# Up projection's moving activations in rows of 272 columns, with single buffers for two of the convolution's tiles

## The chip, the cores and the metric

The kernel runs on one core of one Trainium2 chip. The metric is the device time of one execution in microseconds, as the median of several runs. Before the change it is 1212.79 us (three runs, 1211.92 to 1213.15).

## What is computed

One decoder layer over 272 positions (16 meta tokens and 256 of the sequence), model width 2048, everything in float32. Cut to what matters here:

```
u = rmsnorm(h, norm_mix)
proj = u @ w_in                                  # retention and mLSTM heads
mix = concat([ret, hm]) @ w_out
h = h + mix
u = rmsnorm(h, norm_ffn)
up = causal_dwconv(u @ w_up, ffn_conv_w, ffn_conv_b)   # 3 taps, 2 x 5632 channels
gate, val = split(up)
h = h + (silu(gate) * val) @ w_down
return rmsnorm(h)[:, 16:]
```

The meta tokens are dropped at the end, so the up projection is needed for the last 256 positions and for the two before them that the convolution's three taps reach back to: 258 columns (`NQ = 258`, `T = 272`, `T0 = 14`, `SEQ = 256`).

## The kernel before

**Precision.** A float32 product is made of three passes of TensorE in the type float32r: weights and activations are each parted into a high and a low part, and high by high, high by low and low by high are added up in PSUM. `load_w` (L115) loads a half-tile of weights `wraw` (128 partitions x 8 blocks of 128 columns) by a DMA of SyncE's queue, ScalarE copies it to the high part `whi` (L121) and VectorE subtracts to get the low part `wlo` (L123). There are 4 buffers of `wraw` and 5 each of `whi` and `wlo`.

**A half-tile.** `half_tile` (L135) calls `mmk` (L126): for each of 8 blocks k of the contraction a matmul of `whi` with the high activations (L130) and one with the low ones (L131), and after these sixteen the eight of `wlo` with the high activations (L133). That is 24 matmuls; in each, the weights are the stationary operand (128 x 128) and a row of activations, one row per k, is the moving one. `project` (L140) makes an output tile of 128 channels from two such half-tiles, k = 0 to 7 and k = 8 to 15, in one PSUM bank `mmps` of four.

**Three layouts of moving rows.** The heads read `xh` and `xl`, tiles of shape (128, 16, 272): a row of one k has 272 columns, 1088 bytes. Keys and values use all 272; queries and gates of the retention heads, and the mLSTM gates, use the last 258 (`xh[:, k, 14:272]`). The output projection reads `mixh` and `mixl`, of shape (128, 16, 258), in rows of 1032 bytes. The up projection reads `uh` and `ul` (L567, L568), of the same shape (128, 16, 258).

**Stages.** In the order of time: heads (to about 371 us), output projection (16 tiles, to 465), first half of the up projection (44 tiles, each gate tile followed by its value tile), first half of the down projection, second half of the up projection (44 tiles), second half of the down projection, and the last norm. `out_tile` (L577) writes `uh` (ScalarE, L580) and `ul` (VectorE, L581) row by row while the output projection runs, sixteen times each. The 88 tiles of the up projection are 176 half-tiles.

**Behind each tile of the up projection** runs `conv3` (L630): VectorE takes the tile out of PSUM into `cu` with the norm's factor (L633), ScalarE makes the third tap and the bias from it into `gt` or `vt` (L635), and VectorE adds the two other taps, reading `cu` twice more (L637, two instructions). When gate and value are there, ScalarE applies silu to `gt` (L767), VectorE multiplies by `vt` (L768), and the product is parted for the down projection (L744, L746). `cu`, `gt` and `vt` are tiles of the pool `wk2` with two buffers each. They are named at L631 and L634.

**Order.** Each engine takes its instructions in the order of a schedule that is made when the program is built; waits between engines are semaphores. A tile's buffer may be written again when the last reader of its former content is done. Beside the tiles, GpSimd's queue starts early loads for the down projection (L713 to L722), and VectorE transposes `hT` (L628).

**Where the tiles lie.** The pools `hnp`, `up` and `wk2` are stacked on the right side of the on-chip memory, each below the one before. In every partition `hn` begins at byte 212,960, `ul` at 196,448, `uh` at 179,936; `xh` of the heads lay at 165,760 and `xl` at 183,168, `mixh` at 94,656. Buffers of weights lie 4096 bytes apart.

Of the kernel before, what the change touches and what calls it, by code (L numbers as in the profile page):

```python
# [10 lines left out]
F32 = mybir.dt.float32  # L11
F32R = mybir.dt.float32r
# [4 lines left out]
P = 128  # L17
DM = 2048
KT = DM // P
SEQ = 256  # L20
NMETA = 16
T = SEQ + NMETA
T0 = NMETA - 2
NQ = T - T0
# [59 lines left out]
def trunk(ctx: ExitStack, tc: tile.TileContext, io, out: bass.AP):  # L84
    nc = tc.nc

    def pool(name, bufs, **kw):
        return tc.tile_pool(name=name, bufs=bufs, **kw)
# [13 lines left out]
    def pcol(name, i, n=1):  # L102
        a = _COLS[name][0]
        return par[:, a + i : a + i + n]
# [101 lines left out]
    with pool("sq", 1, side="right") as sqp:  # L206
        for k0, k1 in [(0, 1), (1, 2)] + [(k, k + 2) for k in range(2, KT, 2)]:
            n = k1 - k0
# [355 lines left out]
    hn = hnp.tile([P, 2, DM], F32, name="hn")  # L564
    up_cm = pool("up", 1, side="right")
    up = up_cm.__enter__()
    uh = up.tile([P, KT, NQ], F32R, name="uh")  # L567
    ul = up.tile([P, KT, NQ], F32R, name="ul")  # L568
    wk2_cm = pool("wk2", 2, side="right")
    wk2 = wk2_cm.__enter__()  # L570

# [56 lines left out]
            nc.vector.transpose(dst[:, :, t, 32 * i : 32 * (i + 1)], src[:, :, t, a, :])  # L628

    def conv3(ps, f, name):  # L630
        u = wk2.tile([P, NQ], F32, name="cu")  # L631
        nonlocal evacuated
        evacuated = nc.vector.tensor_tensor(out=u, in0=ps[:, :NQ], in1=rstd2, op=ALU.mult)  # L633
        o = wk2.tile([P, SEQ], F32, name=name)  # L634
        nc.scalar.activation(o, u[:, 2:], AF.Identity, scale=pcol("fw", 3 * f + 2), bias=pcol("fb", f))  # L635
        for j in range(2):
            nc.vector.scalar_tensor_tensor(out=o, in0=u[:, j : j + SEQ], scalar=pcol("fw", 3 * f + j), in1=o, op0=ALU.mult, op1=ALU.add)  # L637
        return o
# [85 lines left out]
    for half in range(2):  # L724
# [23 lines left out]
        gt = None  # L748
        for jj in range(NHF):
            j = half * NHF + jj  # L750
            pair = []
            for s in range(2):
# [7 lines left out]
                if 2 * jj + s in begins:  # L760
                    n = begins.index(2 * jj + s)
                    b, q = units[n]
                    running.append(Early(b, half * NQD + q, homes[n], gt))
                    early[b, q] = running[-1].kept
            gt = conv3(pair[0], j, "gt")
            vt = conv3(pair[1], NF + j, "vt")
            nc.scalar.activation(gt, gt, AF.Silu)  # L767
            nc.vector.tensor_tensor(out=gt, in0=gt, in1=vt, op=ALU.mult)  # L768
# [280 lines left out]
```

## Time and profile before

| | |
|---|---|
| median of three runs | 1212.79 us |
| span of the profiled execution, first to last instruction | 1210.4 us |
| TensorE busy | 1198.6 us, 99% |
| VectorE busy | 970.1 us, 80% |
| ScalarE busy | 708.5 us, 59% |
| GpSimd busy | 165.1 us, 14% |
| output projection, a stretch of 94.00 us | TensorE 94.00, VectorE 61.84, ScalarE 55.76 |
| first half of up, a stretch of 242.90 us | TensorE 242.90, VectorE 209.32, ScalarE 130.73 |
| second half of up, a stretch of 246.30 us | TensorE 246.30, VectorE 194.94, ScalarE 134.66 |

The profile shows one execution; its own time on the device isn't listed beside its span, so the 2.39 us between the median and the span stand for what lies around the span. Durations of single matmuls overlap, because matmuls are pipelined: the time that a matmul takes from the others is the distance from its start to the next start, not its own length. In the views of stretches, the number in brackets behind an engine's busy time counts its instructions.

### The profile page before, as it was taken

What the parts mean: (1) busy time and instruction counts of PE and PEld (TensorE: products, weight loads), DVE (VectorE), ACT (ScalarE), POOL (GpSimd) and SP (SyncE); (2) the same over time, 40 slices, a digit from 0 to 9 for tenths busy, and PEclk for the clock granted to TensorE, in tenths of its full rate; (3) what the DMA queues carried; (4) which work ended last, traced back from release to release, by engine and by line L of the source; (5) the groups of instructions that cost most, each with busy time, mean ns of one, the idle gap of its engine ahead of it and who ended that gap; (6) DMA issues with size and microseconds to landing.
All of it is one profiled execution on the core that took longest, in us unless ns stands there. A gap on an engine that the chain in (4) does not pass through costs nothing.

```text
span 1210.4 us, 22758 instructions
## 1 busy us (share of the span) xinstructions
PE 1198.6 (99%) x8956; PEld 1155.6 (95%) x8956; DVE 970.1 (80%) x1444; ACT 708.5 (59%) x963; POOL 165.1 (14%) x228
## 2 busy tenths in 40 slices
PE   9999999999999999999999999999999999999997
PEld 9999999999999999999999997788999999998886
DVE  8877778766775767789888879996798778789897
ACT  8657646656556656555555546665555555556674
POOL 0100001111110211021122210202022112100232
PEclk9999999999999999999999999999999999999999
DMA  8765555656564655766766775959777677755956
GB/s 277 265 220 160 166 189 171 199 175 189 181 193 141 208 178 176 248 220 208 246 225 209 270 268 202 261 200 272 275 252 261 216 245 239 259 177 208 286 179 185
DMA packets 83004, 263.27 MB, mean 218 GB/s; under 512 B 14672, under 2 KB 18896, under 8 KB 82768
## 3 DMA queue, kind: packets, MB, share of 16 engines
q1 hardware_dynamic: 71952, 223.85, 56.4%
q0 software_dynamic: 10368, 37.11, 10.0%
q8 instruction: 70, 1.15, 0.4%
q10 hardware_dynamic: 576, 0.85, 0.2%
q14 instruction: 38, 0.31, 0.1%
HBM read 243.42 MB, written 11.27 MB: 210 GB/s over the span
## 4 chain that ended last, share of the span: by engine, by line
PE 92%; DMA 4%; DVE 2%; issue 1%; ACT 0%; SPq 0%; DVEq 0%; POOL 0%; ACTq 0%; POOLq 0%
PE mmps L130 25%; PE mmps L131 25%; PE mmps L133 24%; PE atps L807 3%; PE atps L808 3%; PE atps L810 2%; PE mmps L842 2%; PE mmps L839 1%; PE mmps L840 1%; PE atps L842 1%; PE atps L840 1%; PE atps L839 1%; DMA wraw<-in_wd 1%; DMA hT<-in_wd 1%; DVE wlo L746 1%
## 5 line engine op out<-in xcount | busy, mean ns | idle before, releaser
L121 ACT CAST whi<-wraw 128x1024 fp32r<-128x1024 f32 x352 | 368.7, 1049 | 316.6 <-PE mmps L131 216.9
L123 DVE TENSOR_TENSOR wlo<-wraw,whi 128x1024 fp32r<-128x1024 f32 x352 | 433.1, 1232 | 71.9 <-ACT whi L121 69.6
L130 PE MATMUL mmps<-uh,whi 128*128 128x258 f32 x1408 | 346.7, 283 | 0.0
L131 PE MATMUL mmps<-ul,whi 128*128 128x258 f32 x1408 | 346.6, 283 | 0.0
L131 PEld LDWEIGHTS mmps<-ul,whi 128*128 128x128 f32 x1408 | 266.6, 189 | 0.1
L130 PEld LDWEIGHTS mmps<-uh,whi 128*128 128x128 f32 x1408 | 266.4, 189 | 0.1
L130 PE MATMUL mmps<-xh,whi 128*128 128x272 f32 (+2 forms) x864 | 219.9, 288 | 0.0
L131 PE MATMUL mmps<-xl,whi 128*128 128x272 f32 (+2 forms) x864 | 218.4, 286 | 0.0
L133 PE MATMUL mmps<-uh,wlo 128*128 128x258 f32 x1408 | 199.0, 283 | 0.0
L133 PEld LDWEIGHTS mmps<-uh,wlo 128*128 128x128 f32 x1408 | 181.3, 189 | 0.0
L131 PEld LDWEIGHTS mmps<-xl,whi 128*128 128x128 f32 x864 | 163.0, 189 | 0.0
L130 PEld LDWEIGHTS mmps<-xh,whi 128*128 128x128 f32 x864 | 162.7, 188 | 0.1
L133 PE MATMUL mmps<-xh,wlo 128*128 128x272 f32 (+2 forms) x864 | 126.8, 286 | 0.0
L133 PEld LDWEIGHTS mmps<-xh,wlo 128*128 128x128 f32 x864 | 114.4, 188 | 0.0
L633 DVE TENSOR_TENSOR cu<-mmps,rstd 128x258 f32<-128x258 f32 x88 | 37.3, 424 | 47.6 <-PE mmps L133 47.1
L746 DVE TENSOR_TENSOR wlo<-hT,whi 128x1024 fp32r<-128x1024 f32 x52 | 62.8, 1236 | 5.6 <-ACT whi L744 5.0
L744 ACT CAST whi<-hT 128x1024 fp32r<-128x1024 f32 x52 | 53.3, 1051 | 23.4 <-DMA hT<-in_wd 5.6
L131 PE MATMUL mmps<-mixl,whi 128*128 128x258 f32 x256 | 63.0, 283 | 0.0
L130 PE MATMUL mmps<-mixh,whi 128*128 128x258 f32 x256 | 62.4, 283 | 0.0
L744 ACT CAST whi<-wraw 128x1024 fp32r<-128x1024 f32 (+1 forms) x52 | 42.1, 835 | 18.5 <-DVE wraw L824 4.8
L807 PE MATMUL atps<-whi,mh 128*128 128x512 f32 (+1 forms) x132 | 50.9, 387 | 2.0 <-ACT whi L121 2.0
L746 DVE TENSOR_TENSOR wlo<-wraw,whi 128x1024 fp32r<-128x1024 f32 (+1 forms) x52 | 51.4, 1014 | 0.8 <-PE mmps L842 0.2
(276 smaller groups left out, 1704.4 us busy)
## 6 DMA issues: line engine op xcount, KB each, us to landing
wraw<-in_wu SPq DMA_DIRECT2D x176, 512.0 KB, 4.4
wraw<-in_wi SPq DMA_DIRECT2D x108, 512.0 KB, 4.2
hT<-in_wd SPq DMA_DIRECT2D x26, 768.0 KB, 4.5
wraw<-in_wd SPq DMA_DIRECT2D x36, 512.0 KB, 5.1
wraw<-in_wo SPq DMA_DIRECT2D x32, 512.0 KB, 3.8
x<-in_wd POOLq DMA_DIRECT2D x14, 768.0 KB, 7.6
hT<-in_wd POOLq DMA_DIRECT2D x12, 768.0 KB, 6.4
hn<-x POOLq DMA_DIRECT2D x27, 256.0 KB, 7.8
```

The source lines that it names most:

```text
L121: nc.scalar.copy(hi, raw)
L123: nc.vector.tensor_tensor(out=lo, in0=raw, in1=hi.bitcast(F32), op=ALU.subtract)
L130: nc.tensor.matmul(ps, hi[:, k, :], xh(kk), start=kk == first, stop=False)
L131: nc.tensor.matmul(ps, hi[:, k, :], xl(kk), start=False, stop=False)
L133: nc.tensor.matmul(ps, lo[:, k, :], xh(kk), start=False, stop=kk == last)
L633: evacuated = nc.vector.tensor_tensor(out=u, in0=ps[:, :NQ], in1=rstd2, op=ALU.mult)
L744: copied = nc.scalar.copy(hi, x)
L746: return copied, nc.vector.tensor_tensor(out=lo, in0=x, in1=hi.bitcast(F32), op=ALU.subtract)
L807: nc.tensor.matmul(ps, ah[i], hi[:, i, cols], start=first and i == 0, stop=False)
L808: nc.tensor.matmul(ps, al[i], hi[:, i, cols], start=False, stop=False)
L810: nc.tensor.matmul(ps, ah[i], lo[:, i, cols], start=False, stop=last and i == 1)
L842: nc.tensor.matmul(o, sh[:, f, m, :], lo[:, i, :], start=False, stop=end)
```

## The change

Two edits. The first allocates `uh` and `ul` with rows of 272 columns and uses the last 258 of each; every instruction that reads or writes them has the same number of elements as before. The second gives `cu` and `vt` one buffer each; `gt` keeps two.

```
-    uh = up.tile([P, KT, NQ], F32R, name="uh")
-    ul = up.tile([P, KT, NQ], F32R, name="ul")
+    uh, ul = (up.tile([P, KT, T], F32R, name=n)[:, :, T0:] for n in ("uh", "ul"))
...
     def conv3(ps, f, name):
-        u = wk2.tile([P, NQ], F32, name="cu")
+        u = wk2.tile([P, NQ], F32, name="cu", bufs=1)
         nonlocal evacuated
         evacuated = nc.vector.tensor_tensor(out=u, in0=ps[:, :NQ], in1=rstd2, op=ALU.mult)
-        o = wk2.tile([P, SEQ], F32, name=name)
+        o = wk2.tile([P, SEQ], F32, name=name, bufs=2 if name == "gt" else 1)
```

In bytes of each partition: `uh` and `ul` grow from 16,512 to 17,408 each, 1,792 together; a buffer of `cu` (1,056 with its padding) and one of `vt` (1,024) are given back.

## The prediction

> **What bounds the kernel now.** I read the page first: busy time, the slices, the chain of work that ended last.
>
> ```profile
> span 1210.4 us, 22758 instructions
> ...
> PE 1198.6 (99%) x8956; PEld 1155.6 (95%) x8956; DVE 970.1 (80%) x1444; ACT 708.5 (59%) x963; POOL 165.1 (14%) x228
> ...
> PEclk9999999999999999999999999999999999999999
> ...
> PE 92%; DMA 4%; DVE 2%; issue 1%; ACT 0%; SPq 0%; DVEq 0%; POOL 0%; ACTq 0%; POOLq 0%
> PE mmps L130 25%; PE mmps L131 25%; PE mmps L133 24%; PE atps L807 3%; PE atps L808 3%; PE atps L810 2%; PE mmps L842 2%; PE mmps L839 1%; PE mmps L840 1%; PE atps L842 1%; PE atps L840 1%; PE atps L839 1%; DMA wraw<-in_wd 1%; DMA hT<-in_wd 1%; DVE wlo L746 1%
> ```
>
> TensorE has work in 1198.6 of 1210.4 us at a full clock, and three lines, L130, L131 and L133, carry 74% of the chain. A change of any other engine is worth nothing here while TensorE stays fed. So I ask of this change two things only: does the distance from matmul to matmul alter, and does TensorE stay fed. For the second, the busy time of the up projection's two stretches:
>
> ```profile
> core 0: us, PE busy (x) PEld busy (x) DVE busy (x) ACT busy (x) POOL busy (x), PEclk, DMA share, GB/s
> ...
> 474.25:717.15 242.90, 242.90 (x2017) 242.90 (x2016) 209.32 (x322) 130.73 (x176) 46.28 (x70) 1.00 0.70 236
> 840.00:1086.30 246.30, 246.30 (x2045) 246.30 (x2044) 194.94 (x293) 134.66 (x181) 38.23 (x65) 1.00 0.74 245
> ```
>
> TensorE is busy in all of both. VectorE comes next with 209.32 / 242.90 = 86%, then DMA with 70 to 74%. The waits say who runs ahead of whom:
>
> ```profile
> ACT whi L121 <- PE mmps L131: 216.9, 173, 4.2
> ...
> DVE cu L633 <- PE mmps L133: 47.1, 45, 1.6
> ```
>
> ScalarE waits 216.9 us in 173 waits until TensorE has read an older `whi`, so the weights are ready early; VectorE waits for tiles to be finished. Both wait for TensorE, and TensorE for neither.
>
> For the first question I need the pace. The mean length of a matmul (0.28 us in every layout) says nothing, as matmuls overlap. I take the starts: the group of eight L133 weight loads comes once in a half-tile, so from one group's start to another's is a whole number of half-tiles. I laid five stretches from group start to group start and asked for L133 alone:
>
> ```profile
> core 0: us, PE busy (x) PEld busy (x), PEclk, DMA share, GB/s
> 72.89:81.49 8.60, 3.35 (x24) 3.06 (x25) 1.00 0.66 207
> 184.00:186.88 2.88, 1.12 (x8) 1.02 (x8) 1.00 0.63 195
> 406.44:461.16 54.72, 21.35 (x152) 19.59 (x152) 1.00 0.60 190
> 476.06:719.10 243.04, 94.98 (x672) 86.53 (x672) 1.00 0.70 236
> 839.17:1088.00 248.83, 97.24 (x688) 88.59 (x688) 1.00 0.73 243
> ```
>
> The count of matmuls by eight is the number of half-tiles. All five stretches have 258 moving columns and the clock at 1.00, and yet:
> - heads, gates one behind the other (rows of 272, last 258 used): 8.60 / 3 = 2.867 us for a half-tile;
> - heads, a query (the same rows): 2.88;
> - output projection (rows of 258): 54.72 / 19 = 2.880;
> - up, first half (rows of 258): 243.04 / 84 = 2.8933;
> - up, second half: 248.83 / 86 = 2.8934.
>
> The up projection is the slowest of them by 13 to 27 ns in a half-tile, and to four digits equally slow in both of its halves, with DMA and VectorE differently loaded. So it isn't load that slows it. The starts within it show more:
>
> ```profile
> 505.00 1.03 PEld L133 LDWEIGHTS mmps<-uh,wlo 128*128 128x128 f32 x8
> ...
> 507.88 1.03 PEld L133 LDWEIGHTS mmps<-uh,wlo 128*128 128x128 f32 x8
> ...
> 510.78 1.03 PEld L133 LDWEIGHTS mmps<-uh,wlo 128*128 128x128 f32 x8
> ```
>
> 2.88, then 2.90: the half with k = 8 to 15 takes longer than that with k = 0 to 7. Weights, banks and counts are alike in the two; what differs is which rows of `uh` and `ul` are read. The pace hangs on where the moving rows lie.
>
> **The change part by part.**
>
> *Rows of 272 columns.* Nothing is added or removed: 176 half-tiles of 24 matmuls with 258 columns. What moves is the start of each row. With 1032 bytes a row, starts go round a 64-byte block in steps of 8. With 1088 bytes (17 x 64) every start has the same place in it, as in the heads. It is not the heads' place: the tiles end where `hn` begins, so `uh` comes to 212,960 - 2 x 17,408 = 178,144 and its first used column to 178,200, which is 24 in a block of 64; in the heads it is 165,760 + 56, or 56. In a block of 32 the two agree (24). Weights stay where they are.
>
> The trace has no row of this exact layout, so the pace is bounded by the nearest ones. The best is the gates' 2.867: (2.8934 - 2.8667) x 176 = 4.7 us less. In the middle are the heads' query and the output projection with 2.880: (2.8934 - 2.880) x 176 = 2.4 us less. The worst is not bounded by a row of this pitch; all of those are faster than the up projection. I take for the upper end the mirror image of the gates, 2.920, 4.7 us more. I choose the gates' pace, because the gates are the only rows of pitch 272 where three whole half-tiles of 258 columns follow each other without another kind of matmul between, which is how the up projection runs.
>
> [...]
>
> *Writing the rows.* `out_tile` writes 258 columns as before, at another step between rows, beside a busy TensorE. I take 0. If each of the 32 instructions grew by a tenth of its length, that would be about 1.4 and 0.8 us for VectorE and ScalarE, in the output projection's stretch, where both are idle for a third of the time and more:
>
> ```profile
> L581 DVE SCALAR_TENSOR_TENSOR ul<-hT,par,uh 128x258 fp32r<-128x258 f32 x16 | 14.3, 895 | 0.0
> ...
> L580 ACT ACTIVATE uh<-hT,par 128x258 fp32r<-128x258 f32 x16 | 8.2, 511 | 4.3 <-DVE hT L579 4.3
> ```
> ```profile
> core 0: us, PE busy (x) PEld busy (x) DVE busy (x) ACT busy (x) POOL busy (x), PEclk, DMA share, GB/s
> ...
> 371.00:465.00 94.00, 94.00 (x782) 93.89 (x781) 61.84 (x77) 55.76 (x80) 11.54 (x14) 1.00 0.55 178
> ```
>
> *One buffer for `cu`.* L633 may now write only when the former tile's L635 and both L637 have read. These are VectorE's own, in its own queue ahead of L633, except L635, for which L637 waits in any case. One gate and one value tile in order of time:
>
> ```profile
> 495.25 0.60 ACT L635 ACTIVATE gt<-cu,par 128x256 f32<-128x256 f32 x1
> ...
> 500.96 0.60 ACT L635 ACTIVATE vt<-cu,par 128x256 f32<-128x256 f32 x1 [0.34 <-DVE cu L633]
> ```
> ```profile
> 493.65 0.42 DVE L768 TENSOR_TENSOR gt<-gt,vt 128x256 f32<-128x256 f32 x1
> ...
> 496.52 1.00 DVE L637 SCALAR_TENSOR_TENSOR gt<-cu,par,gt 128x256 f32<-128x256 f32 x2
> ...
> 500.50 0.43 DVE L633 TENSOR_TENSOR cu<-mmps,rstd 128x258 f32<-128x258 f32 x1 [1.51 <-PE mmps L133]
> ...
> 501.97 1.00 DVE L637 SCALAR_TENSOR_TENSOR vt<-cu,par,vt 128x256 f32<-128x256 f32 x2
> ...
> 506.28 0.43 DVE L633 TENSOR_TENSOR cu<-mmps,rstd 128x258 f32<-128x258 f32 x1
> ```
>
> The gate's last reading ends at 497.52, the value's L633 starts at 500.50: 2.98 us of slack; the next time 506.28 - 502.97 = 3.31. Cost 0. Were the cover gone, what stands behind L633 on VectorE is the next L123, whose `wlo` TensorE's next eight L133 need; a wait shorter than VectorE's idle time there (1.51) would still be free.
>
> *One buffer for `vt`.* L635 writes it at 500.96, and its last reader, L768, ended at 494.07: 6.9 us of slack. Cost 0; behind it on ScalarE waits the next L121.
>
> *What is late next.* With a half-tile 1% shorter, VectorE's 86% becomes 87%, and DMA's 74% 75%; neither is a bound. The stages behind start sooner by what is saved, with the same distances. I carry all of it to the end.
>
> **The sum.** Span 1210.4 - 4.7 = 1205.7. The runs' median is 2.39 above the span, and I carry that unchanged: 1208.1 us.
>
> **The rivals.** A measurement of this kernel can tell about 0.2% from no change, 2.4 us here.
> - *The pace becomes that of the output projection and of the query, 2.880.* For it: the query reads the very same rows as the gates and doesn't reach their pace, so the layout alone doesn't fix it; the output projection has the old pitch and the same 2.880, so part of the slowness is where the old tiles happened to begin. Against: the gates hold theirs for three half-tiles running. 1212.8 - 2.4 = 1210.4, on the edge of what can be told.
> - *Nothing changes.* The pitch isn't the cause, and the new place is as good as the old: about 2.893 again, 1212.8. For it: the output projection's pitch of 258 and its better pace, and the place of 24 instead of 56. Against: both stretches of pitch 272 above are faster. [...]
> - *Slower: the new place is a bad one.* All 32 rows now share one place in the block; if it is one at which a row takes longer to begin, no row makes up for it, where the old rows went through eight places and were averaged. The slow half shows that groups of rows differ. From 2.907 on it can be measured; at 2.920 it is 1212.8 + 4.7 = 1217.5. Against: two of the three faster stretches have one shared place too.
>
> **How the numbers follow.** Gates' pace 0.45; 2.880 or near it 0.28; nothing 0.18; slower 0.09. The second case lies on the edge and gives a bit over a third of its chance to faster: faster 0.45 + 0.10 = 0.55, same 0.18 + 0.18 = 0.36, slower 0.09. The range reaches from the gates' pace with 0.6 us of spread between runs and as much again for the 0.01 us to which the 8.60 is rounded (1206.9) to no change with a little spread (1213.0); left out are the slower case and the tails, under 2 in 10. The likeliest case alone: 1206.9 to 1209.3.
>
> **What would show it.** Right: the same L133 count, from group start to group start in both stretches, at 2.867 a half-tile and alike for both kinds of half, the up stretches shorter by about 2.3 us each, every other stretch as long as before; no wait of L633 for L635 and none of L635 for L768. Wrong: a pace of 2.88 or above; halves that still differ; TensorE idle between half-tiles; or a gain in the up projection that the down projection's stretches give back.

## The result and the profile after

The changed kernel takes 1215.32 us (median of 20 runs, 1212.85 to 1217.03) against 1212.42 us (20 runs, 1210.22 to 1216.12) of the kernel before; the medians are 2.9 us apart. The ratio is 1.002, 95% interval 1.0012 to 1.0028: slower by about 2.4 us, between 1.5 and 3.4, where 4.7 us less was forecast. One of the five executions with rows at 16 below had a granted clock of 0.556 and took 1949.32 us; its ratio leaves that one out. The changed kernel's profiled execution has a span of 1213.6 us.

The page of the changed kernel, the lines that answer to those of before (span, busy time, clock, chain by engine):

```profile
span 1213.6 us, 22800 instructions
...
PE 1201.3 (99%) x8956; PEld 1157.7 (95%) x8956; DVE 969.9 (80%) x1444; ACT 708.2 (58%) x963; POOL 165.0 (14%) x228
...
PEclk9999999999999999999999999999999999999999
...
PE 93%; DMA 3%; DVE 2%; issue 1%; ACT 0%; DVEq 0%; POOL 0%; ACTq 0%; POOLq 0%
```

As many instructions on every engine, the same granted clock (0.998 as the mean of either profile), VectorE and ScalarE as busy as before; TensorE alone is busy 2.7 us longer. So it isn't a wait that was added; the same matmuls take more time. The stretches from one L133 group's start to another's, in both halves of the up projection (duration, TensorE busy with its count, weight loads, clock, share of DMA and its rate):

```profile
core 0: us, PE busy (x) PEld busy (x), PEclk, DMA share, GB/s
475.92:720.08 244.16, 94.20 (x672) 86.33 (x673) 1.00 0.71 234
838.43:1091.22 252.79, 97.56 (x696) 89.41 (x696) 1.00 0.74 243
```

672 / 8 = 84 half-tiles: 244.16 / 84 = 2.907 us each; 696 / 8 = 87, and 252.79 / 87 = 2.906. Before it was 2.8933 and 2.8934. By the first stretch that is 0.0133 x 176 = 2.3 us more, about what the ratio gives. The group starts one by one, in time order:

```profile
475.92 1.03 PEld L133 LDWEIGHTS mmps<-uh,wlo 128*128 128x128 f32 x8
...
478.82 1.03 PEld L133 LDWEIGHTS mmps<-uh,wlo 128*128 128x128 f32 x8
...
481.73 1.03 PEld L133 LDWEIGHTS mmps<-uh,wlo 128*128 128x128 f32 x8
...
484.64 1.03 PEld L133 LDWEIGHTS mmps<-uh,wlo 128*128 128x128 f32 x8
```

2.90, 2.91, 2.91: the turns of 2.88 and 2.90 are gone (in the trace's full times they were 2.890 and 2.897, and are 2.907 now). With one place for all rows the two kinds of half-tile are alike, as forecast, but alike slow.

For the second edit, what the instructions that read or write `cu` waited for in the changed kernel (us in total, times; L632, L634 and L636 are L633, L635 and L637 of before):

```profile
its engine sat idle before it (us, times) until:
  PE mmps L133: 52.8, 49
  DVE cu L632: 21.6, 48
  POOL x L783: 3.0, 2
  ACT vt L634: 0.8, 1
  ACT gt L634: 0.8, 2
```

L632 waits for TensorE's tiles; ScalarE ends three waits of 1.6 us in all, and those are of the taps that need its result in any case. L634, which writes `vt`, waits for no L767. VectorE waits longer for TensorE than before (52.8 against 47.1 us); with the single buffers alone, at the old pace, it is 51.0, so the pace explains at most a part of that.

### The profile page after: what moved, and what is told of

Its sections match the earlier page's. It is cut to its first block, busy times and chain, and to the rows that moved or that the text cites. A ratio compares the mean times of both kernels' runs of the same rounds, so it can differ in the third digit from the quotient of the medians.

```text
span 1213.6 us, 22800 instructions
## 1 busy us (share of the span) xinstructions
PE 1201.3 (99%) x8956; PEld 1157.7 (95%) x8956; DVE 969.9 (80%) x1444; ACT 708.2 (58%) x963; POOL 165.0 (14%) x228
## 4 chain that ended last, share of the span: by engine, by line
PE 93%; DMA 3%; DVE 2%; issue 1%; ACT 0%; DVEq 0%; POOL 0%; ACTq 0%; POOLq 0%
PE mmps L131 25%; PE mmps L130 25%; PE mmps L133 24%; PE atps L806 3%; PE atps L807 3%; PE atps L809 2%; PE mmps L841 2%; PE mmps L838 2%; PE mmps L839 2%; PE atps L839 1%; PE atps L838 1%; PE atps L841 1%; DMA wraw<-in_wd 1%; DMA x<-in_wd 1%; DVE wlo L745 1%
## 5 line engine op out<-in xcount | busy, mean ns | idle before, releaser
L130 PE MATMUL mmps<-uh,whi 128*128 128x258 f32 x1408 | 350.2, 283 | 0.0
L130 PEld LDWEIGHTS mmps<-uh,whi 128*128 128x128 f32 x1408 | 266.3, 189 | 0.1
L130 PE MATMUL mmps<-xh,whi 128*128 128x272 f32 (+2 forms) x864 | 220.0, 288 | 0.0
L133 PE MATMUL mmps<-uh,wlo 128*128 128x258 f32 x1408 | 197.4, 282 | 0.0
L133 PEld LDWEIGHTS mmps<-uh,wlo 128*128 128x128 f32 x1408 | 180.9, 188 | 0.0
L130 PEld LDWEIGHTS mmps<-xh,whi 128*128 128x128 f32 x864 | 162.9, 188 | 0.1
L133 PE MATMUL mmps<-xh,wlo 128*128 128x272 f32 (+2 forms) x864 | 126.8, 286 | 0.0
L133 PEld LDWEIGHTS mmps<-xh,wlo 128*128 128x128 f32 x864 | 114.4, 189 | 0.0
L632 DVE TENSOR_TENSOR cu<-mmps,rstd 128x258 f32<-128x258 f32 x88 | 37.4, 425 | 53.4 <-PE mmps L133 52.8
L130 PE MATMUL mmps<-mixh,whi 128*128 128x258 f32 x256 | 62.4, 283 | 0.0
```

The source lines that it names most:

```text
L130: nc.tensor.matmul(ps, hi[:, k, :], xh(kk), start=kk == first, stop=False)
L133: nc.tensor.matmul(ps, lo[:, k, :], xh(kk), start=False, stop=kk == last)
```

## Experiments

**The theories.** *Place*: where in a block of 64 bytes the moving rows start sets the pace; 24 is a bad place, and 56, that of the heads, a good one. *Pitch*: rows of 1088 bytes are slow in this region, wherever they start. *Buffers*: the single buffers slow it. Rows of 272 columns leave 14 columns free, so the same tile can be used from another column on, and each two columns move the start by 8 bytes with nothing else changed:

```
-    uh, ul = (up.tile([P, KT, T], F32R, name=n)[:, :, T0:] for n in ("uh", "ul"))
+    uh, ul = (up.tile([P, KT, T], F32R, name=n)[:, :, 6:6 + NQ] for n in ("uh", "ul"))
```

A single execution of the kernel before takes 1210.2 to 1216.1 us, so one execution doesn't tell times that differ by 2 us. The pace does: each of the kernels that were profiled twice, those with rows at 16, 48 and 56 and the one with the single buffers alone, had the same pace both times, to a nanosecond in a half-tile (rows at 16: 237.44 us for 84 half-tiles in both profiles). In the following I go by the pace.

**The heads' place: rows at 56.** The diff above.

> The changed kernel with columns 6 to 264 of the rows of 272 in place of 14 to 272, so that every row of uh and ul starts at 56 in a block of 64 bytes, as in the heads, and not at 24. Place theory (the place of the row's start in a block of 64 sets the pace): a half-tile of the up projection takes 2.867 us as in the heads' gates, not 2.907, and the time falls by 176 x 0.040 = 7.0 us to about 1208.3. Pitch theory (rows of 1088 bytes are slow in this region of the memory, wherever they start): 2.907 again, about 1215. Buffer theory (the single buffers slow it): 2.907 again.

The stretches of this kernel, as above:

```profile
475.91:716.72 240.81, 94.15 (x672) 85.94 (x673) 1.00 0.73 239
836.49:1083.02 246.53, 96.39 (x688) 87.97 (x689) 1.00 0.74 246
```

240.81 / 84 = 2.867 and 246.53 / 86 = 2.867, the pace of the heads' gates, from a shift of 32 bytes. A single execution took 1207.14 us. Place holds; pitch falls, and so do the buffers, which are single here too.

**Rows at 32** (`[:, :, 0:NQ]`).

> The changed kernel with columns 0 to 258 of the rows of 272: every row starts at 32 in a block of 64 bytes. Place theory: a pace of its own, between 2.86 and 2.92 us a half-tile, the same in all half-tiles; a place that is 8 bytes from 24 may be like it. Pitch theory and buffer theory: 2.907.

```profile
476.56:719.32 242.76, 94.63 (x672) 86.72 (x672) 1.00 0.72 236
835.94:1087.06 251.12, 98.89 (x696) 90.48 (x697) 1.00 0.75 245
```

242.76 / 84 = 2.890 and 251.12 / 87 = 2.886; 1213.18 us. A pace of its own, but not quite the same in both stretches. In the trace's full times the half-tiles of the first stretch go by turns of 2.871 and 2.909, and those of the second are at 2.887 throughout. The theory had neither in it.

**Rows at 0** (`[:, :, 8:8 + NQ]`).

> The changed kernel with columns 8 to 266: every row starts at the beginning of a block of 64 bytes. Place theory: a pace of its own between 2.86 and 2.92, the same in all half-tiles. If what costs is only a start that isn't aligned to a block, this is the fastest of the places, at or below 2.867. Pitch theory and buffer theory: 2.907.

```profile
475.95:720.11 244.16, 94.15 (x672) 86.75 (x673) 1.00 0.72 234
```

244.16 / 84 = 2.907, as slow as rows at 24; 1215.01 us. A start aligned to a block isn't best: it is one of the two worst places.

**The buffers alone**, one execution, then timed (the rows of the tiles as before, the second edit kept):

```
-    uh, ul = (up.tile([P, KT, T], F32R, name=n)[:, :, T0:] for n in ("uh", "ul"))
+    uh, ul = (up.tile([P, KT, NQ], F32R, name=n) for n in ("uh", "ul"))
```

> Single buffers for cu and vt alone; uh and ul keep their rows of 258 columns and lie where they lay before. Place theory: the pace of before, 2.893 us a half-tile, 2.88 and 2.90 by turns, and the time of before, about 1212.5. Buffer theory: 2.907 and about 1215.3. In either case no wait of L633 for an L635 and none of L635 for an L768.

> The single buffers alone, timed: pace 2.893 as before and a ratio of 1.000 within 0.001, so that the second edit has no price. If it has one that the pace doesn't show, a ratio of 1.001 or more.

```profile
476.22:719.26 243.04, 94.98 (x672) 86.53 (x673) 1.00 0.72 236
```

243.04 / 84 = 2.8933, to four digits the pace of before. The single execution took 1214.19 us; timed, 1212.8 against 1212.49, a ratio of 1.0004 (0.9996 to 1.0013). The second edit has no price that can be measured.

**Place by itself, or against the weights.** All buffers of weights lie 4096 bytes apart and start at 0 in a block of 64. A tile of 32 bytes ahead of them moves them all to 32 and leaves the activations of heads and up projection in place, while those of the output projection move along with the weights (a line more, so L134 stands for L133):

```
     rstd2 = consts.tile([P, NQ], F32, name="rstd2")
+    nc.vector.memset(consts.tile([P, 8], F32, name="shift"), 0.0)
```

> The changed kernel (rows at 24 in a block of 64) with a tile of 32 bytes, set to zero once and used by nothing, ahead of the weights' buffers, so that all weights start at 32 in a block of 64 and not at 0; uh, ul, xh and xl stay. Absolute place theory (where the moving row starts sets the pace by itself): up projection 2.907 us a half-tile as in the changed kernel, the heads' gates 2.867 as ever. Relative place theory (the moving row's start against the weights' start sets it): the up projection's rows now stand at 24 - 32 = -8, which is 56, and get 2.867; the gates' rows come to 56 - 32 = 24 and get 2.907. The output projection's mixh shifts by the same 32 bytes as the weights: relative 2.880 as before; absolute, something else is possible.

Heads' gates first, then the two stretches of up:

```profile
73.26:81.97 8.71, 3.37 (x24) 3.10 (x25) 1.00 0.72 214
476.51:717.31 240.80, 94.15 (x672) 85.93 (x673) 1.00 0.71 236
836.83:1086.25 249.42, 97.52 (x696) 89.02 (x697) 1.00 0.75 246
```

Up projection 240.80 / 84 = 2.867, gates 8.71 / 3 = 2.903. The two have changed places: the rows of up, untouched at 24, became fast, and those of the gates, untouched at 56, slow. (Of the gates' three half-tiles the first is 2.894 in the trace's full times, behind rows of 272 columns, and the two others are 2.907.) The output projection, where both moved by 32, kept its pace: 54.75 us for the same 19 half-tiles before and here. What counts is where the moving row starts against the weights, in a block of 64. Only one shift of the weights, by 32 bytes, was tried. A single execution took 1210.26 us.

**The other places: 48, 8, 40, 16** (`[:, :, 4:4 + NQ]`, `10:`, `2:` and `12:`).

> The changed kernel with columns 4 to 262, rows at 48 in a block of 64. Place theory: a steady pace of its own. If only the neighbourhood of 56 is fast it is 2.87 to 2.88; if pace goes by the distance from the end of the block, between 2.867 (56) and 2.889 (32). Pitch theory is out since the row at 56 was fast.

> The changed kernel with columns 10 to 268, rows at 8 in a block of 64. Place theory: as 0 and 24 both take 2.907, the places between them are slow too and this one takes 2.907.

> The changed kernel with columns 2 to 260, rows at 40 in a block of 64. Place theory: between those of 32 (2.889) and 56 (2.867).

> The changed kernel with columns 12 to 270, rows at 16 in a block of 64, the last of the eight places. Place theory: its own steady pace; its neighbours have 2.874 (8) and 2.907 (24), so between 2.87 and 2.91.

The first stretch of up in each, in this order:

```profile
475.72:715.96 240.24, 93.21 (x672) 85.36 (x673) 1.00 0.72 238
```
```profile
475.74:717.10 241.36, 94.74 (x672) 86.70 (x672) 1.00 0.73 238
```
```profile
475.86:716.66 240.80, 93.02 (x672) 85.97 (x673) 1.00 0.71 235
```
```profile
476.03:713.47 237.44, 93.04 (x672) 84.91 (x673) 1.00 0.71 238
```

With 84 half-tiles in each, all eight places:

| place of the row against the weights | 0 | 8 | 16 | 24 | 32 | 40 | 48 | 56 |
|---|---|---|---|---|---|---|---|---|
| us a half-tile, first stretch | 2.907 | 2.873 | 2.827 | 2.907 | 2.890 | 2.867 | 2.860 | 2.867 |

Single executions: 1207.32 us (48), 1207.52 (8), 1211.36 (40), 1203.38 (16). Three expectations missed: 48 is faster than either of the ranges that I gave it, 8 isn't slow though it lies between two slow places, and 16, beside the slow 24, is the fastest of all, below its range. There is no slope from place to place; each has to be measured.

A pace in the table is a mean over both halves of an output tile. With rows at 48 the two still differ, though all rows have one place in a block of 64:

```profile
478.56 1.02 PEld L133 LDWEIGHTS mmps<-uh,wlo 128*128 128x128 f32 x8
...
481.44 1.01 PEld L133 LDWEIGHTS mmps<-uh,wlo 128*128 128x128 f32 x8
...
484.28 1.02 PEld L133 LDWEIGHTS mmps<-uh,wlo 128*128 128x128 f32 x8
```

2.88, then 2.84 (2.873 and 2.847 in full times), throughout both stretches. So the place in a block of 64 isn't all that counts. The two halves read other rows, and the first one's first matmul overwrites the bank to which the second one adds; no run separates these.

**A test of the rule forward:** rows at 16 and weights at 32 (both edits).

> Rows at 16 and the weights shifted by 32 bytes. Relative place theory: 16 - 32 = -16, which is 48 in a block of 64, so the up projection gets the pace of the kernel with rows at 48, 2.86 us a half-tile by turns of 2.851 and 2.869, whatever rows at 16 give with unshifted weights; the heads' gates are at 24 relative to the weights and take 2.907 again. Absolute place theory: the pace of rows at 16, and gates at 2.867.

```profile
72.94:81.65 8.71, 3.37 (x24) 3.10 (x24) 1.00 0.63 199
476.14:716.38 240.24, 93.22 (x672) 85.35 (x672) 1.00 0.71 234
```

240.24 us for 84 half-tiles, to the last digit the stretch of rows at 48, and not the 237.44 of rows at 16; the gates are at 2.903 again. The relative place foretold the pace. It didn't foretell the time: a single execution took 1213.02 us, 5.7 more than that of rows at 48. Between the two halves' groups, in the first down projection, it is 2.2 us longer (120.7 against 118.4), and behind the last group 3.0 (125.3 against 122.3); why isn't known.

**Timed: rows at 48, 56 and 16.**

> The kernel with rows at 48, timed. Its up projection has 2.860 us a half-tile against 2.893 before, 176 x 0.033 = 5.8 us: about 1206.6 against 1212.4 before, a ratio of 0.995, if nothing is given back behind the up projection. If the stages behind give it back, a ratio of 0.999 or above.

> The kernel with rows at 56, the heads' place, timed. 176 x 0.0265 = 4.7 us less than before: about 1207.7, a ratio of 0.996; about 1 us more than the kernel with rows at 48.

> Rows at 16, timed. The up projection has 2.827 us a half-tile against 2.893, 176 x 0.0665 = 11.7 us less. If all of it arrives: about 1200.3 against 1212, a ratio of 0.990. If some 2 us are given back in the first down projection, as rows at 48 and 56 seem to: about 1202.5, a ratio of 0.992.

| rows at | less by pace alone, us | median, us | before beside it, us | ratio, 95% interval |
|---|---|---|---|---|
| 48 | 5.9 | 1208.13 | 1211.75 | 0.9969 (0.9952 to 0.9985) |
| 56 | 4.7 | 1210.25 | 1211.75 | 0.9983 (0.9970 to 0.9996) |
| 16 | 11.7 | 1204.44 | 1212.49 | 0.9928 (0.9914 to 0.9941) |

All three are faster than the kernel before, rows at 16 by the most. But in each, by the ratios, some 2 to 3 us of the pace's gain don't arrive, and in none does the interval reach that gain. Rows at 56 missed their forecast of about 1207.7 us by this. Where they go, by the timed kernel with rows at 16:

```profile
475.87:713.31 237.44, 93.03 (x672) 84.93 (x673) 1.00 0.73 240
835.11:1078.21 243.10, 95.24 (x688) 86.96 (x689) 1.00 0.75 250
```

From the last group of the first stretch to that of the second it is 1078.21 - 713.31 = 364.90 us, and 1088.00 - 719.10 = 368.90 before: 4.0 less, of which the second stretch's 88 half-tiles should give 88 x 0.0667 = 5.9. So in this pair of profiles 1.9 us are given back between, in the first down projection. The pair can't bear much: from the last group of one half to the first of the other it is 117.2 us before and 119.0 here, but 116.9 and 119.8 in the two profiles of one kernel, that with rows at 56. There VectorE's first subtraction for the down projection (L823, L824 of before) waits for a tile that was worked out early, kept in DRAM and loaded again; before, and in the two profiles with rows at 16, the timed one first:

```profile
DVE wraw L824 <- DMA hT<-kept: 2.5, 1, 2.5
```
```profile
DVE wraw L823 <- DMA hT<-kept: 3.7, 1, 3.7
```
```profile
DVE wraw L823 <- DMA hT<-kept: 2.6, 1, 2.6
```

The longer wait doesn't repeat. The experiment takes it up all the same.

**The early loads a projection sooner**, on top of rows at 16:

```
-            begins = [2 + 4 * i for i in range(9)] + [36, 37, 38, 40, 41]
+            begins = [2 + 4 * i for i in range(9)] + [36, 37, 38, 39, 40]
```

> Rows at 16, and the last two early loads of the first half started one projection (5.7 us) sooner each, at the projections 39 and 40 and not 40 and 41. Theory of the early loads (their chain of transfers ends after the up projection and holds the first down projection up): the first wait of the first down projection for a kept tile, 2 to 4 us before, goes or shrinks, the first down projection takes 112 us or less, and the time falls by 2 us or more below that of rows at 16 alone. Rival (chance, or VectorE's full queue there): the first down projection stays at 113 to 117 us and the time is the same within 1 us.

It took 1208.02 us, a ratio of 0.9954 (0.9941 to 0.9968), slower than rows at 16 alone, which neither the theory nor its rival had in it. The wait for kept tiles did shrink:

```profile
DVE wraw L823 <- DMA hT<-kept: 1.5, 2, 1.0
```

But the schedule's order changed with the edit, on GpSimd's queue and behind it; TensorE was idle for part of the time from 715 to 750 us, and its granted clock fell (busy time of all engines, clock):

```profile
core 0: us, PE busy (x) PEld busy (x) DVE busy (x) ACT busy (x) POOL busy (x), PEclk, DMA share, GB/s
715.00:740.00 25.00, 21.19 (x84) 16.30 (x83) 22.27 (x29) 12.49 (x17) 0.54 (x1) 0.93 0.60 196
740.00:750.00 10.00, 9.42 (x34) 7.61 (x35) 9.36 (x10) 7.04 (x8) 0.00 (x0) 0.83 0.39 142
```

With rows at 16 alone TensorE was busy for 22.63 us of the first of these stretches and 10.00 of the second, and the clock stayed at 1.00 in both. From group to group the first down projection takes 4.2 us longer here (123.2 against 119.0). An estimate from the clock, 0.07 x 25 + 0.17 x 10 = 3.5 us, covers most of that. So the time doesn't bear out that this chain alone holds the first down projection up, and doesn't refute it either; with an unchanged order and clock it stays open. The same profile shows a second thing, in the stretches of up:

```profile
475.62:713.06 237.44, 93.03 (x672) 84.93 (x673) 1.00 0.73 238
836.23:1085.05 248.82, 97.13 (x696) 88.44 (x697) 1.00 0.75 247
```

237.44 / 84 = 2.827 in the first half, 248.82 / 87 = 2.860 in the second, with the same rows, the same places and the same clock. One place has more than one steady pace. The slower half is 87 x 0.033 = 2.9 of the 6.4 us by which this profile's span is longer than that of rows at 16 alone (1207.4 against 1201.0).

## Why the prediction was wrong, point by point

**What bounds the kernel: right.** TensorE's pace sets the time; 2.3 us more in 176 half-tiles account for the 2.4 us that the ratio gives, and the busy time of VectorE and ScalarE changed by 0.3 us at most.

**That the pace hangs on where the moving rows lie: right**, and shown: 32 bytes of shift are worth 2.907 against 2.867. The turns from which it was read aren't explained by this, though. Rows of 1032 bytes take each half-tile of before through all eight places, in both kinds of half. By the table, averaged as the third rival had it, that would be 2.875 us; it was 2.893, and the two kinds differed by 7 ns. What slowed the old rows stays open.

**The choice of the gates' pace: the step that failed.** I had worked out that the rows would start at 24 and not at 56, and put this aside because the two agree in a block of 32 and because the gates were the nearest stretch without other matmuls between. A block of 32 isn't enough: 24 and 56 are 40 ns apart in a half-tile, so that the term of 4.7 us less came out as 2.3 us more. (Blocks larger than 64 weren't told apart: rows of 1088 bytes take each place through both halves of 128.) The gates' pace was right for rows like the gates', as the kernel with rows at 56 shows; it was the wrong row to take for these. With a place that no row of the trace had, the forecast should have been the whole spread of paces and more, not one end of it: the prediction says itself that no row bounds the slow side, and its range still ends at no change.

**"Weights stay where they are": true, and it hid the second half of the rule.** A moving row has no good place by itself; moving the weights by 32 bytes turned good and bad round. The heads and the up projection had the same weights' buffers, so the profile of before couldn't show it.

**The rival on the slower side was the right one**, with a bad place shared by all rows; that a row takes longer to begin there is shown by no run. Its price, 2.920, was the mirror image of the gates' pace and not read from a row; the measured one is 2.907. That 2.907 stands in the rival, as the pace from which a loss can be measured, is a coincidence. It had a chance of 0.09. Against it I had put that the stretches with one shared place were faster; they shared another place.

**The rival of no change: wrong.** The new place isn't as good as the old ones were: 2.907 us in a half-tile against 2.893. With the place as the one thing changed, the distance from one matmul's start to the next goes from 2.827 / 24 = 117.8 to 2.907 / 24 = 121.1 ns. Rows at 8 and at 24 are 34 ns apart in a half-tile (2.873 and 2.907).

**The single buffers at nothing: right** (1.0004, and the pace unchanged). **Writing the rows at nothing: right**: the output projection's stretch holds the same work.

```profile
371.00:465.00 94.00, 94.00 (x783) 93.89 (x782) 61.56 (x77) 55.78 (x80) 11.51 (x14) 1.00 0.56 177
```

**That all of a gain is carried to the end: wrong in size.** It couldn't be seen in the changed kernel, but of 11.7 us with rows at 16 some 8.7 arrive (0.0072 x 1212.5; between 7.2 and 10.4 by the interval). In the pair of profiles compared, 1.9 us are lost in the first down projection, no more than that stretch varies between two profiles of one kernel; where and by what the gain is lost is open.

**Two small readings.** The 2.39 us around the span compare a median with the span of another execution. Where both are on record for one execution they are 1.8 us apart (1215.4 and 1213.6). And the group that ends the output projection's stretch of nineteen half-tiles starts at 461.18 and not 461.16, which makes its pace 2.881. Neither moves the forecast by more than 0.6 us.

## What to carry to other kernels

In this kernel, where TensorE is the bound, the start of the moving rows against the stationary operand's was a free setting of some 3% of a matmul's distance (117.8 to 121.1 ns). In one like it, try the eight places of 8 bytes in a block of 64 before believing in any of them, and count half-tiles from group start to group start, since the mean length of a matmul doesn't show the distance: at L130 in the up projection it is 283 ns before and after, while the distance went from 2.8933 / 24 = 120.6 to 2.907 / 24 = 121.1 ns. When a row of the trace is borrowed as a price, compare everything that isn't the same, the other operand's address too; a difference that seems too small to matter is the thing to put into the range. And a place measured today can be lost with the next tile that is put in front of either operand, as the 32 bytes ahead of the weights show (the gates' half-tile went from 2.867 to 2.903 us with them).

## What the runs showed of the hardware

- 258 float32r columns at the full clock: 117.8 to 121.1 ns from start to start, for the most part set by the moving row's place against the weights' in a block of 64 bytes, with no order from place to place (table above). It isn't set by that alone: at 48 the two halves of a tile take 2.873 and 2.847 us.
- The same rows and places may run at more than one steady pace: 2.827 and 2.860 in the two halves of one kernel with rows at 16, turns of 2.871 and 2.909 and then a steady 2.887 in those of the kernel with rows at 32. Each held for the rest of its stretch. What chooses it isn't known. In the first case the clock had fallen before the second half (0.93 and 0.83 from 715 to 750 us); in the second case it stood at 1.00 in both stretches.
- With TensorE busy for 21.19 of the 25 us from 715 to 740, its granted clock was 0.93 in that stretch and 0.83 in the next ten; with 22.63 of the same 25, in the kernel with rows at 16 alone, it stayed at 1.00. What lowered it isn't known.
